# Cross-attention queries as seven half-size block products per head, attention behind all four heads, values by both token tiles per piece

## The chip, the core and the metric

The kernel runs on one core of a Trainium2 chip. Its time is device microseconds. A core has TensorE (matrix products, "PE" in the profile, its weight loads "PEld"), VectorE ("DVE"), ScalarE ("ACT"), GpSimd ("POOL") and SyncE ("SP", which issues most DMAs); the engines run side by side and wait for one another by semaphores. Matrix products go to PSUM, which VectorE and ScalarE read; everything else lies in SBUF.

## The reference

One encoder layer on 512 tokens of width 1024, all in float32, with three parts that each add to x, and a final norm:

```python
x = x + hybrid_mixer(rms_norm(x, norm_mix_g), ...)
x = x + memory_cross_attention(rms_norm(x, norm_xa_g), mem, mem_norm_g, w_q_xa, w_k_xa, w_v_xa, w_o_xa)
x = x + swiglu(rms_norm(x, norm_ffn_g), w_gate_ffn, w_up_ffn, w_down_ffn)
return rms_norm(x, final_g)
```

The change is in the second part. There are 256 memory tokens and 4 heads of 256 columns:

```python
m = rms_norm(mem, mem_g)
q, k, v = h @ wq, m @ wk, m @ wv              # h: 512 x 1024, m: 256 x 1024, weights 1024 x 1024
s = einsum("bqhd,bkhd->bhqk", q, k) * 256 ** -0.5
o = einsum("bhqk,bkhd->bqhd", softmax(s), v)
return o @ wo
```

## The kernel before

**Numbers.** A float32 operand is cut into two parts of a reduced format, a high one (a copy on ACT) and a low one (the rest, a subtraction on DVE); `split` (L101) does it. A product is then three matmul passes, high x high, high x low, low x high (`gemm`, L137). Weights arrive as raw tiles of 1 MB by a DMA on SP's queue into a ring of three (`load_raw`, L111) and are cut into a ring of six pairs (`cut`, L116).

**Order.** Tokens are in four tiles of 128. Instructions are put in order by a planner that works with estimated times; among those ready it goes by the order in which the code writes them. Instructions wrapped in `pin` (L233) keep their written order among themselves on their engine; others may be moved between them.

**Seven products.** The gate projections of the mixer and the gate and up projections of the feed-forward part already use a scheme with seven half-size block products in place of eight (`Seven`, L235, and `seven_run`, L311). An item is 256 weight columns by 512 tokens. Its weights are cut in two along input and output, its activations along input and tokens. The sums of weight blocks are made for each item (two on POOL in `sums`, two on DVE in `sums2`), those of activation blocks once (`r11`, `r21`, `r22` are plain blocks, `t1` to `t4` sums). A product (`mul`, L274) is 12 matmuls of 256 columns. Two accumulators in PSUM take several products one after the other, and copies of states in between (`keep`, L284, on ACT: m1, u2, u3) are added on DVE to give the four blocks of the output: `c11`, `c22`, `c12`, `c21`. `seven_run` is a pipeline over items: in step k it issues five products of item n = k and the last two of item p = k - 1, and prepares the weights of item q = k + 1. All of it is pinned. The accumulators are tiles of a ring of four ("acc"); an item takes two.

**Cross-attention.** After the mixer's output product (`bo`, a `Back`, L853, which leaves normed tokens in `hs`), `norm_turn` (L197) transposes each token tile on PE, multiplies by the gain on DVE and cuts the result into `h2`. Keys go by four loads of 256 columns (L940 to L947), values by two halves of 512 columns through `nat_gemm` (L150), which runs all four pieces of a half for the first token tile and then for the second. Then, head by head, `xa_q` (L958) makes the queries by 48 matmuls of 512 columns and cuts them with the scale, `xa_turn` (L992) transposes the head before, `xa_probs` (L968) makes scores, maximum, exponential and division, `xa_values` (L1001) the weighted values. The output product `bx` starts behind the last head's scores, with that head's transposes and values between its rows.

**Feed-forward.** The tokens are cut into four quarter tiles per part (`h3q`, read through `Quads`, L1037), and the seven-product items of gate and up follow.

Of the kernel before, what the change touches and what calls it, by code (L numbers as in the profile page):

```python
# [8 lines left out]
F32 = mybir.dt.float32  # L9
# [8 lines left out]
def encoder_kernel(  # L18
# [9 lines left out]
    nc = tc.nc  # L28
# [46 lines left out]
    WB = 6  # L75
    chan = cst.tile([P, NC_], F32, name="chan")
    cst.tile([P, 48], F32, name="cpad")
    sm.tile([P, 48], F32, name="spad", bufs=1)
# [155 lines left out]

    class Seven:  # L235


        def __init__(self, src, fp, rights, tile_a):
            self.src, self.fp, self.r, self.tile_a = src, fp, rights, tile_a
# [6 lines left out]
        def sums(self):  # L246

            r = self.raw
            self.s1 = self.fp.tile([P, 4, P], F32, name=nm("s1"), tag="s1", bufs=1)
            pin(nc.gpsimd.tensor_tensor(out=self.s1, in0=r[:, 0:4, P:256], in1=r[:, 4:8, P:256], op=ALU.add))  # L250
            pin(nc.gpsimd.tensor_tensor(out=r[:, 0:4, P:256], in0=r[:, 0:4, 0:P], in1=r[:, 0:4, P:256], op=ALU.subtract))  # L251

        def sums2(self):

# [56 lines left out]
    def seven_run(items, fill=lambda i: None, at=None, then=None):  # L311

        z = len(items)
        for k in range(z + 1):
            n = items[k] if k < z else None
            p = items[k - 1] if k else None
            q = items[k + 1] if k + 1 < z else None
            if k == at:
                got = then()
            if k + 2 < z:  # L320
                items[k + 2].load()
            if n:
# [12 lines left out]
            if p:  # L335
                p.gate22()
                p.mul(p.c, "s4", "r22", False, True)
            if k == z:
                fill(1)
            if q:  # L340
                x = q.hi(("l11", "l12"), q.left)
                q.lo(x)
                c = q.hi(("s1",), q.s1)
            if p:
                p.c12(p.c[:, 0:256], p.u2)
            if n:
# [36 lines left out]
        if z > 1:  # L383
            items[z - 1].extra_out()
        return got if then else None
# [277 lines left out]
    def sgu_v(t, dst):  # L663
        zt = up.tile([P, W], F32, name=nm("zt"), tag="zt", bufs=2)
        nc.scalar.activation(out=zt, in_=dst, func=AF.Gelu)
        st = sm.tile([P, 6], F32, name=nm("st"), tag="st")
        nc.vector.bn_stats(out=st, in_=zt)
        mv = sm.tile([P, 2], F32, name=nm("mv"), tag="mv")
# [184 lines left out]
    class Back:  # L853
# [42 lines left out]
        def half1(self, during=lambda t: None):  # L896
# [3 lines left out]
            for t in range(NT):  # L900
# [3 lines left out]
                    self.step(1, i, t)  # L904
                self.finish(1, t)

    for t in range(NT):
# [42 lines left out]
    close(mp)  # L950
    close(n2)
    close(mtp)


    op_ = pool("op", side="right")
    oT = tuple(op_.tile([P, KD, T], F32R, name=f"oT{s}") for s in "hl")
    qp = pool("qp", side="right")

    def xa_q(h):
        tiles = w_cols(w_q_xa, h * XD)  # L960
        qx = tuple(qp.tile([P, 2, T], F32R, name=nm("qx"), tag=f"qx{s}", bufs=2) for s in "hl")
        for j in range(2):
            dst = bank(nm("pq"))
            col_gemm(dst, tiles[j], h2, ALLT)
            split(dst, qx[0][:, j, :], qx[1][:, j, :], scale=XD ** -0.5)
        return qx

    def xa_probs(h, qx):  # L968
        es = qp.tile([P, NT, NM], F32, name=nm("es"), tag="es", bufs=1)
        for tt in range(2):  # L970
            sc = bank(nm("sc"))
            for u in range(2):
                t = 2 * tt + u
                gemm(sc[:, u * NM:(u + 1) * NM],
                     lambda i: qx[0][:, i, t * P:(t + 1) * P], lambda i: qx[1][:, i, t * P:(t + 1) * P],
                     lambda i: kx[0][:, 2 * h + i, :], lambda i: kx[1][:, 2 * h + i, :], [(0, 0), (1, 1)])
            mx = sm.tile([P, 2], F32, name=nm("mx"), tag="mx")
            nc.vector.tensor_reduce(out=mx, in_=sc.rearrange("p (u m) -> p u m", u=2), axis=AX.X, op=ALU.max)
            nc.vector.tensor_scalar(out=mx, in0=mx, scalar1=-1.0, scalar2=None, op0=ALU.mult)
            su = sm.tile([P, 2], F32, name=nm("su"), tag="su")  # L980
            for u in range(2):
                nc.scalar.activation(out=es[:, 2 * tt + u, :], in_=sc[:, u * NM:(u + 1) * NM], func=AF.Exp,
                                     bias=mx[:, u:u + 1], accum_out=su[:, u:u + 1])
            ri = sm.tile([P, 2], F32, name=nm("ri"), tag="ri")
            nc.vector.reciprocal(out=ri, in_=su)
            for u in range(2):
                t = 2 * tt + u
# [1 line left out]
                                        op0=ALU.mult)  # L989
        return es  # L990

    def xa_turn(es):  # L992
        pT = tuple(qp.tile([P, MT, T], F32R, name=nm("pT"), tag=f"pT{s}", bufs=2) for s in "hl")
        for m in range(MT):
            dst = bank(nm("pT"))
            for t in range(NT):
# [12 lines left out]
    XH = D // XD  # L1009
# [12 lines left out]
    bx.rows(0, 2, 6)  # L1022
    xa_values(XH - 1, pT)
    close(qp)
    close(h2p)
    close(kvp)

    h3p = pool("h3p")
    h3q = [[[None, None] for _ in range(2)] for _ in range(2)]
    for at in ((0, 1, 0), (0, 1, 1), (1, 1, 0), (1, 1, 1), None, (0, 0, 0), (0, 0, 1), (1, 0, 0), (1, 0, 1)):  # L1030
        if at is None:
            h3p.tile([P, 48], F32, name="hpad")
        else:
            u, v, w = at
            h3q[u][v][w] = h3p.tile([P, 4, T // 2], F32R, name=f"h3{'hl'[w]}{u}{v}", tag=f"h3{'hl'[w]}{u}{v}")

    class Quads:  # L1037
        def __init__(self, s):
            self.s = s

        def __getitem__(self, at):
            p, k, c = at
            k, k1 = (k.start, k.stop) if isinstance(k, slice) else (k, None)
            b = c.start // (T // 2)
            c = slice(c.start - b * (T // 2), c.stop - b * (T // 2))
            return h3q[k // 4][b][self.s][p, k % 4 if k1 is None else slice(k % 4, k1 - k + k % 4), c]

    h3 = (Quads(0), Quads(1))
# [425 lines left out]
```

## Time and profile before

| | us |
|---|---|
| median of 3 runs | 961.09 (959.71 to 961.42) |
| the profiled execution, its own time | 961.33 |
| its span, first to last instruction | 959.4 |
| PE busy in the span | 943.3 (98%) |
| DVE busy | 691.9 (72%) |
| ACT busy | 485.4 (51%) |
| POOL busy | 235.2 (25%) |

The span is what the engines' rows cover; the execution's own time holds 1.93 us more around it. A group's row gives line, engine, operation, tiles, shapes and count, then busy time, the mean of one in nanoseconds, and the idle time before. A row of the timeline begins with start and length in microseconds. Matmuls overlap in the pipe, so the time that one costs is read from the distance of starts and not from its length.

### The profile page before, as it was taken

The page shows a single profiled execution, that of the slowest core. Times are in us where ns is not written, and L with a number is a line of the kernel's source. Part 1 is how long each engine was busy: PE and PEld are TensorE (multiplying, and loading weights), DVE is VectorE, ACT ScalarE, POOL GpSimd, SP SyncE. Part 2 cuts the span into 40 slices and gives each one's busy share as a digit, 9 for nine tenths or more (in the row PEclk, how much of TensorE's full clock was granted, in tenths as well). Part 3 has the DMA queues.
Part 4 walks back from the last instruction along what each step waited for, and adds up shares of the span by engine and source line. Part 5 has one row for each costly group of instructions (what it writes and reads, how often), then busy time and mean ns, then how long its engine had stood idle before and what let it go on. Part 6 is the DMA issues. An engine that isn't in the chain of part 4 may idle for free. (4 is left out here: it accounts for less than half of the span.)

```text
span 959.4 us, 14493 instructions
## 1 busy us (share of the span) xinstructions
PE 943.3 (98%) x5894; PEld 849.7 (89%) x5894; DVE 691.9 (72%) x863; ACT 485.4 (51%) x746; POOL 235.2 (25%) x211
## 2 busy tenths in 40 slices
PE   7999999999999999999999999999999999999996
PEld 7988888888999999988988888899999999988885
DVE  6677887658966666566844544598888888777996
ACT  6474665434544344455734433555455545557452
POOL 1221122254411535230000000034544545201001
PEclk8999999999999999999999999999999999999999
DMA  8421212320333323282545121112424242376632
GB/s 289 148 91 44 88 55 78 121 88 22 111 100 120 110 89 110 89 283 67 176 136 172 44 88 44 44 45 89 132 89 133 88 132 89 111 263 138 235 110 87
DMA packets 84275, 109.22 MB, mean 114 GB/s; under 512 B 2177, under 2 KB 63665, under 8 KB 84209
## 3 DMA queue, kind: packets, MB, share of 16 engines
q1 hardware_dynamic: 82384, 101.74, 32.3%
q0 software_dynamic: 1824, 6.55, 2.6%
q8 instruction: 46, 0.75, 0.3%
q14 instruction: 21, 0.16, 0.1%
HBM read 104.10 MB, written 2.10 MB: 111 GB/s over the span
## 5 line engine op out<-in xcount | busy, mean ns | idle before, releaser
L272 DVE TENSOR_TENSOR wl<-wr,wh 128x1024 fp32r<-128x1024 f32 x93 | 135.7, 1470 | 29.4 <-ACT wh L267 29.4
L105 DVE TENSOR_TENSOR wl<-wr,wh 128x1024 fp32r<-128x1024 f32 x80 | 99.7, 1255 | 58.5 <-ACT wh L104 32.7
L104 ACT CAST wh<-wr 128x1024 fp32r<-128x1024 f32 x80 | 82.9, 1050 | 65.8 <-PE pq L142 20.8
L267 ACT CAST wh<-wr 128x1024 fp32r<-128x1024 f32 x93 | 97.8, 1053 | 25.4 <-DVE wr L257 25.4
L174 POOL TENSOR_TENSOR rs<-ve,mhalf 128x1 f32<-128x1 f32 x22 | 14.9, 679 | 304.7 <-DVE ve L172 304.7
L286 ACT COPY u<-pf 128x256 f32<-128x256 f32 x62 | 23.1, 373 | 94.3 <-PE pf L280 31.9
L250 POOL TENSOR_TENSOR s<-wr 128x512 f32<-128x512 f32 x31 | 40.7, 1314 | 115.2 <-DVE w L272 111.1
L251 POOL TENSOR_TENSOR wr<-wr 128x512 f32<-128x512 f32 x31 | 64.6, 2085 | 2.4
L806 POOL TENSOR_TENSOR merged<-merged,sg 128x512 f32<-128x512 f32 x16 | 27.5, 1723 | 79.9 <-DVE sg L805 79.9
L582 POOL TENSOR_SCALAR_AFFINE_SELECT ab<-ab 128x128 f32<-128x128 f32 x32 | 23.8, 777 | 80.1 <-ACT ab L579 80.1
L280 PE MATMUL pf<-h3th,wh 128*128 128x256 f32 x240 | 37.5, 279 | 0.4 <-ACT m L286 0.4
L280 PE MATMUL pf<-h3th,wl 128*128 128x256 f32 x240 | 37.0, 276 | 0.0
L280 PE MATMUL pf<-h3tl,wh 128*128 128x256 f32 x240 | 37.0, 276 | 0.0
L286 ACT COPY m<-pf 128x256 f32<-128x256 f32 x31 | 11.5, 372 | 47.3 <-PE pf L280 45.1
L280 PEld LDWEIGHTS pf<-h3th,wh 128*128 128x128 f32 x240 | 32.2, 189 | 0.7 <-ACT m L286 0.6
L280 PEld LDWEIGHTS pf<-h3tl,wh 128*128 128x128 f32 x240 | 31.7, 188 | 0.0
L280 PEld LDWEIGHTS pf<-h3th,wl 128*128 128x128 f32 x240 | 31.7, 188 | 0.0
L257 DVE TENSOR_TENSOR wr<-wr 128x512 f32<-128x512 f32 x31 | 30.2, 975 | 1.1
L1201 ACT CAST wh<-wr 128x1024 fp32r<-128x1024 f32 x20 | 20.7, 1051 | 18.3 <-PE pc L1170 8.4
L183 ACT ACTIVATE jk<-xr 128x512 f32<-128x512 f32 x24 | 15.2, 631 | 25.6 <-DVE xr L886 13.0
L1127 POOL TENSOR_TENSOR afb<-afb,g 128x256 f32<-128x256 f32 (+1 forms) x16 | 18.4, 1153 | 35.0 <-DVE afb L1100 35.0
L805 DVE TENSOR_TENSOR sg<-pbr,sg 128x512 f32<-128x512 f32 x16 | 11.0, 689 | 20.8 <-PE pbr L798 20.8
(385 smaller groups left out, 2674.8 us busy)
## 6 DMA issues: line engine op xcount, KB each, us to landing
wr<-in_w_in_dram SPq DMA_DIRECT2D x26, 1024.0 KB, 5.1
wr<-in_w_down_ffn_dram SPq DMA_DIRECT2D x13, 1024.0 KB, 5.5
wr<-in_w_gate_ffn_dram SPq DMA_DIRECT2D x11, 1024.0 KB, 5.4
wr<-in_w_up_ffn_dram SPq DMA_DIRECT2D x11, 1024.0 KB, 5.4
wb<-in_w_branch_dram SPq DMA_DIRECT2D x12, 512.0 KB, 3.4
wr<-in_w_out_dram SPq DMA_DIRECT2D x4, 1024.0 KB, 8.2
wr<-in_w_k_xa_dram SPq DMA_DIRECT2D x4, 1024.0 KB, 8.0
wr<-in_w_v_xa_dram SPq DMA_DIRECT2D x4, 1024.0 KB, 5.1
```

The costliest lines, as they stand in the source:

```text
L104: nc.scalar.copy(out=hi, in_=src)
L105: nc.vector.tensor_tensor(out=lo, in0=src, in1=hi, op=ALU.subtract)
L250: pin(nc.gpsimd.tensor_tensor(out=self.s1, in0=r[:, 0:4, P:256], in1=r[:, 4:8, P:256], op=ALU.add))
L251: pin(nc.gpsimd.tensor_tensor(out=r[:, 0:4, P:256], in0=r[:, 0:4, 0:P], in1=r[:, 0:4, P:256], op=ALU.subtract))
L257: pin(nc.vector.tensor_tensor(out=r[:, 4:8, 0:P], in0=r[:, 4:8, 0:P], in1=r[:, 0:4, 0:P], op=ALU.subtract))
L267: pin(nc.scalar.copy(out=t[0], in_=src))
L272: pin(nc.vector.tensor_tensor(out=l, in0=src, in1=h, op=ALU.subtract))
L280: pin(nc.tensor.matmul(dst[:, 0:256], w[:, k, :], v[:, k, :], start=first and n == 0, stop=last and n == 11, skip_group_check=True))
L286: pin(nc.scalar.copy(out=m, in_=self.a[:, 0:256]))
L582: nc.gpsimd.affine_select(out=dg, in_=dg, compare_op=ALU.is_gt, fill=0.0, base=0, channel_multiplier=1, pattern=[[-1, P]])
L806: pin(nc.gpsimd.tensor_tensor(out=merged[:, d, :], in0=merged[:, d, :], in1=sg, op=ALU.add))
L1201: pin(nc.scalar.copy(out=hi, in_=src))
```

## The change

Queries become four items of the seven-product scheme (`Query`, one per head), run by `seven_run`. For that the normed tokens are kept in quarter tiles `h2q` (a function `quads`, which now also makes `h3q`); the plain block r12 isn't needed in cut form, and its tiles hold the raw block first and then the items' weight sums. `query_turn` takes the place of `norm_turn`, and `query_forms`, called for token tiles 2 and 3, makes the sums t1 to t4 into `h2t`. The outputs of an item are copied (`put`) and later cut (`rest`) into `qx`, one pair of tiles per head; the scale 256 ** -0.5 moves into the exponential. In `seven_run`, the copy u2 is written behind `sums2`, and a new step `out12` (empty for the other classes) follows it. The run's two fill places, ahead of the last two products, hold the scores of heads 0 and 1; heads 2 and 3, all transposes and all values follow the run, and rows of the output product stand between the last two heads' parts. The value projection runs both token tiles for each piece of weights, and the first two heads' loads and head 0's preparation are written behind the second half's matmuls. Probabilities and their transposes lie in tiles of `h2p` that are free by then. A pad and some small buffers become smaller.

```diff
@@ class Seven, seven_run
+        eng = nc.gpsimd
...
-        extra_cut = extra_mul = extra_out = extra_load
+        extra_cut = extra_mul = extra_out = out12 = extra_load
...
             if n:
                 n.mul(n.a, "s2", "t2", False, False)
-                n.u2 = n.keep("u2")
             if q:
                 q.sums2()
+            if n:
+                n.u2 = n.keep("u2")
+            if p:
+                p.out12()
+            if q:
                 q.lo(c)
@@ tokens
-    h2 = tuple(h2p.tile([P, KD, T], F32R, name=f"h2{s}") for s in "hl")
+    h2q = quads(h2p, "h2", F32)
...
-    bo.half1(lambda t: t > 0 and norm_turn(n2, hs[t - 1], G_XA, h2, t - 1))
+    def query_turn(t):
+        i, ts = t // 2, slice(t % 2 * P, (t % 2 + 1) * P)
+        for g in range(2):
...
+            hf = n2.tile([P, 4, P], F32, name=nm("hf"), tag="hf", bufs=2) if i else h2q[0][1][g][:, :, ts]
...
+            nc.vector.tensor_tensor(out=hf, in0=pt.rearrange("p (j c) -> p j c", j=4), in1=gv, op=ALU.mult)
+            if g or not i:
+                split(hf, *(v[:, :, ts] for v in h2q[g][i]))
+
+    def query_forms(t):
+        f = n2.tile([P, 2, 4, P], F32, name=nm("h"), tag="h", bufs=2)
...
+        for n, (p, q, o) in enumerate(((r12, r11, r22), (r22, r12, r21))):
+            if n:
+                nc.vector.tensor_tensor(out=f[:, 1], in0=o, in1=f[:, 1], op=ALU.subtract)
+            nc.vector.tensor_tensor(out=f[:, 0], in0=p, in1=q, op=ALU.subtract)
+            if not n:
+                nc.vector.tensor_tensor(out=f[:, 1], in0=o, in1=f[:, 0], op=ALU.subtract)
...
+            split(f, h2t[0][sl], h2t[1][sl])
+
+    bo.half1(lambda t: t > 0 and query_turn(t - 1))
...
+    query_forms(NT - 2)
@@ keys
         if c == 1:
-            norm_turn(n2, hs[NT - 1], G_XA, h2, NT - 1)
+            query_turn(NT - 1)
+            query_forms(NT - 1)
@@ queries
+    acc = lambda: psm.tile([P, 512], F32, name=nm("pf"), tag="acc", bufs=4)
...
+    class Query(Seven):
...
+        def put(self, j, i, src):
+            hi, lo = (v[:, j, HT[i]] for v in qx[self.h])
+            pin(nc.scalar.copy(out=hi, in_=src))
+            self.due[j, i] = (lo, src, hi)
+        def rest(self, j, i):
+            lo, src, hi = self.due.pop((j, i))
+            pin(nc.vector.tensor_tensor(out=lo, in0=src, in1=hi, op=ALU.subtract))
+        def c11(self, p, m):
+            self.add(p, m)
+            self.put(0, 0, m)
+        def c22(self, p, m):
+            self.add(p, m)
+            self.rest(0, 0)
+            self.put(1, 1, m)
+        def gate22(self):
+            self.rest(1, 1)
+        def c12(self, p, m):
+            self.add(p, m)
+            self.m12 = m
+        def out12(self):
+            self.put(0, 1, self.m12)
+        def done0(self):
+            self.rest(0, 1)
+        def c21(self, p):
+            self.put(1, 0, p)
+        def extra_mul(self):
+            self.rest(1, 0)
@@ values and the order behind them
-    for cs in HALVES:
-        nat_gemm(w_v_xa, cs.start, mT, MT, lambda t, dst: split(dst, vx[0][:, t, cs], vx[1][:, t, cs]))
+    for n, cs in enumerate(HALVES):
+        dsts = [bank(nm("pn")) for t in range(MT)]
+        for c in range(2):
+            for i, pc in enumerate(w_rows(w_v_xa, 4 * c, 4, cs.start)):
+                k = 4 * c + 2 * i
+                for t in range(MT):
+                    gemm(dsts[t],
...
+                         [(k, 0), (k + 1, 1)], first=k == 0, last=k == KD - 2)
+        if n:
+            seven_open(qs)
...
-    es = xa_probs(0, xa_q(0))
-    for h in range(1, XH):
-        qx = xa_q(h)
-        nT = xa_turn(es)
-        es = xa_probs(h, qx)
-        xa_values(h - 1, nT)
+    seven_run(qs, probs)
...
+    turn(0)
+    probs(2)
+    xa_values(0, pT[0])
+    turn(1)
+    probs(3)
+    xa_values(1, pT[1])
     bx.start()
     bx.rows(0, 0, 2)
-    pT = xa_turn(es)
-    bx.rows(0, 2, 6)
-    xa_values(XH - 1, pT)
+    turn(2)
+    bx.rows(0, 2, 4)
+    xa_values(2, pT[2])
+    turn(3)
+    bx.rows(0, 4, 6)
+    xa_values(3, pT[3])
```

More of the change, by code (lines that the diff above doesn't have):

```diff
@@ L249, in sums @@
             self.s1 = self.fp.tile([P, 4, P], F32, name=nm("s1"), tag="s1", bufs=1)
-            pin(nc.gpsimd.tensor_tensor(out=self.s1, in0=r[:, 0:4, P:256], in1=r[:, 4:8, P:256], op=ALU.add))
-            pin(nc.gpsimd.tensor_tensor(out=r[:, 0:4, P:256], in0=r[:, 0:4, 0:P], in1=r[:, 0:4, P:256], op=ALU.subtract))
+            pin(self.eng.tensor_tensor(out=self.s1, in0=r[:, 0:4, P:256], in1=r[:, 4:8, P:256], op=ALU.add))
+            pin(self.eng.tensor_tensor(out=r[:, 0:4, P:256], in0=r[:, 0:4, 0:P], in1=r[:, 0:4, P:256], op=ALU.subtract))
         def sums2(self):
@@ L905, in half1, with quads, __init__, __getitem__ @@
                 self.finish(1, t)
+    def quads(p, name, first=F32R):
+        q = [[[None, None] for _ in range(2)] for _ in range(2)]
+        for at in ((0, 1, 0), (0, 1, 1), (1, 1, 0), (1, 1, 1), None, (0, 0, 0), (0, 0, 1), (1, 0, 0), (1, 0, 1)):
+            if at is None:
+                p.tile([P, 48], F32, name=f"{name}pad")
+            else:
+                u, v, w = at
+                n = f"{name}{'hl'[w]}{u}{v}"
+                q[u][v][w] = p.tile([P, 4, T // 2], first if v > u else F32R, name=n, tag=n)
+        return q
+    class Quads:
+        def __init__(self, q, s):
+            self.q, self.s = q, s
+        def __getitem__(self, at):
+            p, k, c = at
+            k, k1 = (k.start, k.stop) if isinstance(k, slice) else (k, None)
+            b = c.start // (T // 2)
+            c = slice(c.start - b * (T // 2), c.stop - b * (T // 2))
+            return self.q[k // 4][b][self.s][p, k % 4 if k1 is None else slice(k % 4, k1 - k + k % 4), c]
     for t in range(NT):
@@ L946, in encoder_kernel @@
         if c == 1:
-            norm_turn(n2, hs[NT - 1], G_XA, h2, NT - 1)
-    for cs in HALVES:
-        nat_gemm(w_v_xa, cs.start, mT, MT, lambda t, dst: split(dst, vx[0][:, t, cs], vx[1][:, t, cs]))
[L950 to L966, printed above, removed]
@@ L968, in xa_probs, with tile @@
-    def xa_probs(h, qx):
-        es = qp.tile([P, NT, NM], F32, name=nm("es"), tag="es", bufs=1)
+            query_turn(NT - 1)
+            query_forms(NT - 1)
+    XH = D // XD
+    class Room:
+        def tile(self, shape, dtype, name, tag, bufs):
+            if tag == "s1":
+                return h2p.tile(shape, dtype, name=name, tag="h2h01")
+            if tag == "w2h":
+                self.both = h2p.tile([shape[0], 2] + shape[1:], dtype, name=name, tag="h2l01")
+                return self.both[:, 0]
+            if tag == "w2l":
+                return self.both[:, 1]
+            return fq.tile(shape, dtype, name=name, tag=tag, bufs=2)
@@ new lines, in encoder_kernel, with __init__, add @@
+    acc = lambda: psm.tile([P, 512], F32, name=nm("pf"), tag="acc", bufs=4)
+    qrights = dict(r11=h2q[0][0], r21=h2q[1][0], r22=h2q[1][1])
+    for i, n in enumerate((1, 2, 3, 4)):
+        qrights[f"t{n}"] = tuple(v[:, i] for v in h2t)
+    class Query(Seven):
+        def __init__(self, h):
+            super().__init__(w_q_xa[:, h * XD:(h + 1) * XD], room, qrights, acc)
+            self.h, self.due = h, {}
+        def put(self, j, i, src):
[5 more added lines that the diff above has]
+            pin(nc.vector.tensor_tensor(out=lo, in0=src, in1=hi, op=ALU.subtract))
+        def add(self, p, m):
+            pin(nc.vector.tensor_tensor(out=m, in0=p, in1=m, op=ALU.add))
+        def c11(self, p, m):
[18 more added lines that the diff above has]
+            self.rest(1, 0)
@@ L970, in xa_probs @@
+    room = Room()
+    qs = [Query(h) for h in range(XH)]
+    SC = XD ** -0.5
+    def xa_probs(h):
+        es = h2p.tile([P, NT, NM], F32, name=nm("es"), tag=f"h2{'hl'[h % 2]}00")
         for tt in range(2):
@@ L974, in xa_probs @@
                 gemm(sc[:, u * NM:(u + 1) * NM],
[L975 removed]
+                     lambda i: qx[h][0][:, i, t * P:(t + 1) * P], lambda i: qx[h][1][:, i, t * P:(t + 1) * P],
                      lambda i: kx[0][:, 2 * h + i, :], lambda i: kx[1][:, 2 * h + i, :], [(0, 0), (1, 1)])
[L977 removed]
+            mx = sm.tile([P, 2], F32, name=nm("mx"), tag="mx", bufs=3)
             nc.vector.tensor_reduce(out=mx, in_=sc.rearrange("p (u m) -> p u m", u=2), axis=AX.X, op=ALU.max)
[L979 to L980 removed]
+            nc.vector.tensor_scalar(out=mx, in0=mx, scalar1=-SC, scalar2=None, op0=ALU.mult)
+            su = sm.tile([P, 2], F32, name=nm("su"), tag="su", bufs=3)
             for u in range(2):
                 nc.scalar.activation(out=es[:, 2 * tt + u, :], in_=sc[:, u * NM:(u + 1) * NM], func=AF.Exp,
[L983 to L984 removed]
+                                     bias=mx[:, u:u + 1], scale=SC, accum_out=su[:, u:u + 1])
+            ri = sm.tile([P, 2], F32, name=nm("ri"), tag="ri", bufs=3)
             nc.vector.reciprocal(out=ri, in_=su)
@@ L990, in xa_probs, with xa_turn @@
         return es
-    def xa_turn(es):
-        pT = tuple(qp.tile([P, MT, T], F32R, name=nm("pT"), tag=f"pT{s}", bufs=2) for s in "hl")
+    def xa_turn(h, es):
+        pT = tuple(h2p.tile([P, MT, T], F32R, name=nm("pT"), tag=f"h2{s}{1 if h % 2 else 0}1") for s in "hl")
         for m in range(MT):
@@ L1007, in xa_values, with probs, turn @@
             split(dst, oT[0][:, dt_, :], oT[1][:, dt_, :])
-    XH = D // XD
-    es = xa_probs(0, xa_q(0))
-    for h in range(1, XH):
-        qx = xa_q(h)
-        nT = xa_turn(es)
-        es = xa_probs(h, qx)
-        xa_values(h - 1, nT)
+    ess = {}
+    def probs(h):
+        ess[h] = xa_probs(h)
+    for n, cs in enumerate(HALVES):
[5 more added lines that the diff above has]
+                    gemm(dsts[t],
+                         lambda a: mT[0][:, a, t * P:(t + 1) * P], lambda a: mT[1][:, a, t * P:(t + 1) * P],
+                         lambda a: pc[0][:, a, :], lambda a: pc[1][:, a, :],
+                         [(k, 0), (k + 1, 1)], first=k == 0, last=k == KD - 2)
+        if n:
+            seven_open(qs)
+        for t in range(MT):
+            split(dsts[t], vx[0][:, t, cs], vx[1][:, t, cs])
+    close(mp)
+    close(n2)
+    qxp = pool("qxp")
+    qx = [tuple(qxp.tile([P, 2, T], F32R, name=f"qx{s}{h}") for s in "hl") for h in range(XH)]
+    fq = pool("fq")
+    seven_run(qs, probs)
+    close(fq)
+    close(h2tp)
+    op_ = pool("op", side="right")
+    oT = tuple(op_.tile([P, KD, T], F32R, name=f"oT{s}") for s in "hl")
+    pT = {}
+    def turn(h):
+        pT[h] = xa_turn(h, ess[h])
     h3p_done = {}
     bx = Back(w_o_xa, oT, KD, KD, lambda t, half: h3p_done["f"](t, half))
+    turn(0)
[4 more added lines that the diff above has]
+    xa_values(1, pT[1])
     bx.start()
     bx.rows(0, 0, 2)
-    pT = xa_turn(es)
-    bx.rows(0, 2, 6)
-    xa_values(XH - 1, pT)
-    close(qp)
+    turn(2)
[4 more added lines that the diff above has]
+    xa_values(3, pT[3])
+    close(qxp)
     close(h2p)
@@ L1028, in encoder_kernel @@
     h3p = pool("h3p")
[L1029 to L1048, printed above, removed]
+    h3q = quads(h3p, "h3")
+    h3 = tuple(Quads(h3q, i) for i in range(2))
     h3t = tuple(h3p.tile([P, 4, 4, T // 2], F32R, name=f"h3t{s}") for s in "hl")
```

20 lines of the change are left out of this document (17 added, 3 removed).

## The prediction

> **What bounds the kernel now.** I read the page's busy line first, then the busy time of each engine in the stretches that the change touches (columns: stretch, length, then busy time and instructions of PE, PEld, DVE, ACT, POOL, the granted clock, the DMA share, GB/s), then PE's waits there.
>
> ```profile
> span 959.4 us, 14493 instructions
> PE 943.3 (98%) x5894; PEld 849.7 (89%) x5894; DVE 691.9 (72%) x863; ACT 485.4 (51%) x746; POOL 235.2 (25%) x211
> ...
> 461.00:485.75 24.75, 24.75 (x209) 24.75 (x208) 19.68 (x28) 15.77 (x25) 1.40 (x1) 1.00 0.58 190
> 485.75:507.50 21.75, 21.75 (x98) 18.03 (x97) 8.18 (x9) 6.84 (x10) 0.00 (x0) 1.00 0.52 171
> 507.50:594.40 86.90, 86.38 (x441) 73.24 (x440) 44.33 (x78) 37.15 (x72) 0.00 (x0) 1.00 0.26 85
> ...
> PE sc L142 <- DVE qx L108: 0.5, 1, 0.5
> ```
>
> TensorE is busy through keys (461 to 485.75), values (to 507.5) and attention (to 594.4), at full clock; its only wait there is 0.5 us before one score. VectorE (DVE) is half idle in the last stretch. So time is won here only by fewer matmul columns, and lost by any new TensorE wait. The profiled execution took 961.33 us, 1.93 more than its span and 0.24 above the median of 961.09; the sum is made against 961.33 and 0.24 is taken off at the end.
>
> **The products.** Today four heads of queries take 192 matmuls of 512 columns. Their price is the spacing of their starts, since durations overlap. First the queries, then the feed-forward stage, which already runs seven half-size products per item, then the keys, the slowest 256-column product near by:
>
> ```profile
> L142 PE MATMUL pq<-h2h,wl 128*128 128x512 f32 x64 | 16.0, 390 | 0.0
> ...
> 541.32 1.98 PE L142 MATMUL pq<-h2l,wh 128*128 128x512 f32 x8
> 543.13 1.98 PE L142 MATMUL pq<-h2h,wl 128*128 128x512 f32 x8
> ```
> ```profile
> 685.48 0.62 PE L280 MATMUL pf<-h3th,wl 128*128 128x256 f32 x4
> 685.93 0.62 PE L280 MATMUL pf<-h3h,wh 128*128 128x256 f32 x4
> ...
> 695.53 0.62 PE L280 MATMUL pf<-h3h,wh 128*128 128x256 f32 x4
> ```
> ```profile
> 475.19 1.12 PE L142 MATMUL pk<-mTl,wh 128*128 128x256 f32 x8
> 476.15 1.12 PE L142 MATMUL pk<-mTh,wl 128*128 128x256 f32 x8
> ```
>
> Eight 512-column matmuls take 543.13 - 541.32 = 1.81 us, so a head takes 6 x 1.81 = 10.88 us and four take 43.5. An item of seven products (84 matmuls) takes 695.53 - 685.93 = 9.60 us; four take 38.4. **Saved: 5.1 us.** At the keys' pace (0.96 us for eight, 0.12 each) an item would take 10.08 and the saving be 3.2; that is the lower bound. I take 9.60, because the new query tiles are cut into the same quarters as that stage's. Scores, transposes, values and the output product keep their matmuls. The old 0.5 us wait goes too, since its query is long ready when the scores come: **0.5 saved**.
>
> **Work that moves and is hidden.** Each of the two calls of query_forms adds four 128x512 subtractions and two 128x1024 cuts on DVE. Their prices, and when the keys' weights are cut and needed:
>
> ```profile
> 627.99 0.68 DVE L223 TENSOR_TENSOR tf<-hf,hf 128x512 f32<-128x512 f32 x1
> ...
> L105 DVE TENSOR_TENSOR wl<-wr,wh 128x1024 fp32r<-128x1024 f32 x16 | 19.4, 1222 | 9.3 <-ACT wh L104 9.3
> L105 DVE TENSOR_TENSOR h2l<-hf,h2h 128x512 fp32r<-128x512 f32 x6 | 4.1, 687 | 0.1
> ...
> 473.74 1.23 DVE L105 TENSOR_TENSOR wl<-wr,wh 128x1024 fp32r<-128x1024 f32 x1 [0.97 <-ACT wh L104]
> ```
> ```profile
> 482.87 1.12 PE L142 MATMUL pk<-mTh,wh 128*128 128x256 f32 x8
> ```
>
> 4 x 0.68 + 2 x 1.22 = 5.2 us a call, 10.3 in all; two 0.7 us cuts of the block that is no longer needed go. Head 0's preparation adds two subtractions, one half-size cut and one full cut, 3.3 us. DVE has 46.5 - 19.68 - 8.18 = 18.6 us free from 461 to 507.5 and is asked for 12.2 more. The last key weights are cut at 473.74 and first read at 482.87, nine microseconds ahead, so the delay shows nowhere. Taking both token tiles per piece of the value weights gives each piece 12 matmuls, 2.7 us, instead of 1.36 us, so late cuts are excused there too. I price all this at nothing; without the cover it is at most the 3.8 us by which 19.68 + 10.3 - 1.4 overruns the keys' 24.75. The loads on SP's queue are the same four of 1 MB, asked for earlier. The two extra sums a head on GpSimd (POOL) meet an idle engine.
>
> **The new wait.** Each step of the pinned run ends on DVE with: add for c11 (head n), add for c22 (head n), cut of block 00 (head n), and only then, in extra_mul, the cut of block 10 of head n-1, which reads that head's first accumulator in PSUM. There are four such buffers and each head takes two, so the first product of head n+1 reuses exactly that buffer and waits for that last cut. TensorE's pinned order has nothing after product s3t3 to do meanwhile. In the feed-forward stage the accumulator is read earlier. Its rows around the same place (the step begins at 685.93), with the busy times of that step first:
>
> ```profile
> 685.93:695.53 9.60, 9.60 (x86) 9.60 (x85) 8.34 (x11) 4.49 (x7) 5.49 (x4) 1.00 0.36 109
> ...
> 684.77 1.93 DVE L272 TENSOR_TENSOR wl<-wr,wh 128x1024 fp32r<-128x1024 f32 x1 [0.52 <-ACT wh L267]
> 686.63 0.41 DVE L1100 TENSOR_TENSOR af<-pfb,m 128x256 f32<-128x256 f32 x1
> 687.56 0.42 DVE L1100 TENSOR_TENSOR af<-pf,u 128x256 f32<-128x256 f32 x1 [0.52 <-ACT u L286]
> ```
> ```profile
> 687.15 0.37 ACT L286 COPY u<-pf 128x256 f32<-128x256 f32 x1 [2.13 <-DVE af L1100]
> 687.42 1.06 ACT L267 CAST wh<-wr 128x1024 fp32r<-128x1024 f32 x1
> ```
>
> The shortest chain, DVE being on time: s3t3's last matmul ends at 685.48 + 0.62 = 686.10, 0.17 after the point where the next product could start; ACT copies u3 (0.37), then DVE adds c22, cuts 00, cuts 10 (0.34, 0.34, 0.42 with starts overlapping by 0.08), and three hops of about 0.05 to 0.1 (0.04 from ACT's end at 687.52 to DVE at 687.56): 1.8 us. But DVE is late here already: the c11 add begins 0.70 behind the step. Then the copy for block 00 (ACT, 0.37) comes ahead of u3's copy on ACT, and the chain runs 0.70 + 0.41 + 0.3 + 0.4 + 0.34 + 0.34 + 0.42 + hops = 3.0 us. Step 0 holds only five products, 5/7 x 9.60 = 6.9 us, while DVE has nearly the 8.34 us of a whole step to do; I put 0.8 for the part of that lag that is still there at head 2. So head 2 waits 1.8 to **3.8 us**; I take 3.8, as the queue runs late in the nearest rows. At head 3 DVE has had that pause to catch up: **1.8**. Head 1 takes unused buffers, and after head 3 the scores come. Together 5.6.
>
> Can anything fill it? The score matmuls of head 0 aren't pinned, and unpinned work does pass work written earlier in this kernel: scores start between two query products, and the first up-product's multiplication (L1156) stands ahead of a pinned cut that the code writes before it:
>
> ```profile
> 518.42 0.40 PE L142 MATMUL sc<-kxh,qx 128*128 128x256 f32 x2
> 518.65 2.00 PE L142 MATMUL pq<-h2h,wh 128*128 128x512 f32 x8
> ...
> 647.02 0.69 DVE L1156 TENSOR_TENSOR af<-pf,g 128x512 f32<-128x512 f32 x1 [0.39 <-PE pf L142]
> 647.63 1.46 DVE L272 TENSOR_TENSOR wl<-wr,wh 128x1024 fp32r<-128x1024 f32 x1
> ```
>
> At head 2's wait, the scores of head 0's last two token tiles are ready: 12 x 0.12 = 1.4 us, brought forward at no cost. At head 3's, the rest of head 0's are, which covers 1.8. So 3.8 - 1.4 = **2.4 us** of waiting stays, between 0 (if DVE is on time) and 5.6 (if nothing is brought forward).
>
> **Attention behind the queries.** A block of scores goes through a maximum, two exponentials and two scalings before its transposes:
>
> ```profile
> L978 DVE TENSOR_REDUCE mx<-sc 128x2 f32<-128x512 f32 x8 | 5.5, 692 | 13.6 <-PE sc L142 13.6
> L988 DVE TENSOR_SCALAR es<-es,ri 128x256 f32<-128x256 f32 x16 | 4.9, 351 | 0.1
> ```
> ```profile
> L982 ACT ACTIVATE es<-sc,mx 128x256 f32<-128x256 f32 x16 | 7.4, 471 | 15.5 <-DVE mx L979 15.5
> ```
>
> That is 0.69 + 2 x 0.47 + 2 x 0.35 = 2.3 us and some small steps. Score work of two heads (24 x 0.12 = 2.9 us each) and two products of 1.36 lie between head 0's first score and its transposes, 8.5 us; behind them each head's transposes are followed by another head's scores before its values. Nothing waits, as now: 0, with the old 0.5 as upper bound.
>
> **Sum:** -5.1 - 0.5 + 2.4 = -3.2, so 961.33 - 3.2 = 958.1, and 957.9 as a median.
>
> **The rivals.** (1) *Nothing fills the waits*: -5.1 - 0.5 + 5.6 = 0, 961.1. For it: the queue is pinned by hand; against it: the overtaking above. (2) *The unfilled wait slows the clock*, slower than before. The start of this kernel shows what a pause does: PE waited 3.8 us, and the clock (third figure from the right) fell.
>
> ```profile
> 8.00:12.00 4.00, 0.16 (x2) 0.12 (x1) 3.37 (x4) 3.56 (x8) 0.00 (x0) 0.79 1.08 362
> 12.00:16.00 4.00, 4.00 (x19) 4.00 (x20) 4.00 (x9) 2.97 (x5) 0.93 (x1) 0.50 0.77 262
> 16.00:20.00 4.00, 4.00 (x32) 4.00 (x32) 2.50 (x7) 2.65 (x9) 0.09 (x1) 0.86 1.02 327
> ...
> PE pv L142 <- ACT hTh L104: 3.8, 1, 3.8
> ```
>
> Lost: 4 x 0.50 + 4 x 0.14 = 2.6 us. Head 2's wait of 3.8 is as long; with this behind it, rival (1) becomes 963.7. It decides from a wait somewhere between 0.5 us (the one before the scores, at a clock of 1.00) and 3.8; against it: the fill shortens the wait to 2.4. [...] (3) *Everything is covered*: DVE on time, waits of 1.8 wholly filled: -5.6, 955.5. Against it: DVE's rows stand late. (4) *Slow columns*: the keys' 0.12 for the new products; -3.2 - 0.5 + 2.4 = -1.3, 959.8. For it: the same shape does run at two paces.
>
> **How the numbers follow.** Forecast 0.45 (own range 956.4 to 959.2), (1) 0.20, (2) 0.14, (3) 0.12, (4) 0.09. A measurement of this kernel can tell about 0.2%, 1.9 us, from no change; so 959.2 divides faster from same and 963.0 same from slower. Faster: forecast and (3), 0.56; same: (1), (4) and the forecast's edge, 0.28; slower: 0.16. The range runs from 955.3, just below (3), to 963.2, which leaves out most of (2).
>
> **What would show it.** Four items of about 9.6 us, 84 matmuls each, under the queries' line; PE idle before the first product of heads 2 and 3, released by DVE's block-10 cut; scores of head 0 inside the query run; no PE idle from 461 to 507. Wrong if PE doesn't wait there, if the products run near 0.12, if the clock dips behind the wait, or if keys or values wait on their cuts.

## The result and the profile after

The changed kernel takes 953.93 us (median of six runs, 953.23 to 954.58). The kernel before took 960.17 in six runs, of which the three shown ahead of the prediction were 961.09 in the median. The ratio is 0.9933, 95% interval 0.992 to 0.9945: faster by 6.2 us, and the slowest of the new runs (954.58) is below the fastest of the old (959.71). The forecast was 957.9 with a range down to 955.3, so the time lies 4.0 below the forecast and 1.4 below the range. The profiled execution of the changed kernel took 953.87 us.

The busy line of the changed kernel, and then all of PE's waits from 455 to 618 us in it:

```profile
span 952.2 us, 14860 instructions
PE 935.4 (98%) x6038; PEld 849.3 (89%) x6038; DVE 720.6 (76%) x909; ACT 498.5 (52%) x776; POOL 248.6 (26%) x219
```
```profile
PE pf L282 <- DVE qxl L1043: 0.2, 1, 0.2
```

TensorE is still the engine that sets the time, and the forecast's 2.4 us of waiting are 0.2. The same three stretches as before, by engine (columns as in the prediction), show that DVE did take up the work that moved (16.96 us busy in the second stretch, 8.18 before) and that PE has no idle time in the first two:

```profile
461.00:485.75 24.75, 24.75 (x200) 23.96 (x199) 22.79 (x33) 15.78 (x24) 1.39 (x1) 1.00 0.67 210
485.75:507.50 21.75, 21.75 (x115) 18.55 (x114) 16.96 (x19) 9.97 (x15) 6.38 (x4) 1.00 0.31 100
507.50:594.40 86.90, 86.64 (x600) 79.61 (x600) 63.33 (x116) 47.59 (x100) 7.01 (x4) 1.00 0.30 98
```

To compare the two, I measure one stretch in each: from the first key product to the feed-forward part's first product. PE's timeline, before:

```profile
460.99 0.88 PE L142 MATMUL pk<-mTh,wh 128*128 128x256 f32 x6
624.38 1.07 PE L142 MATMUL pf<-h3h,wh 128*128 128x256 f32 x7
```

and after, with three more places that are used below:

```profile
459.85 0.88 PE L142 MATMUL pk<-mTh,wh 128*128 128x256 f32 x6
...
478.20 0.63 PE L142 MATMUL pn<-wh,mTh 128*128 128x512 f32 x2
...
482.40 1.09 PE L142 MATMUL pk<-mTh,wh 128*128 128x256 f32 x8
...
522.14 0.62 PE L282 MATMUL pf<-h2h,wh 128*128 128x256 f32 x4
...
523.50 0.39 PE L142 MATMUL sc<-kxh,qxh 128*128 128x256 f32 x2
...
526.02 0.72 PE L282 MATMUL pf<-h2th,w 128*128 128x256 f32 x4 [0.15 <-DVE qxl L1043]
...
617.18 1.07 PE L142 MATMUL pf<-h3h,wh 128*128 128x256 f32 x7
```

The stretch took 624.38 - 460.99 = 163.39 us and takes 617.18 - 459.85 = 157.33: **6.06 less**, nearly all of the 6.24 between the medians. Summing the distances from each PE row's start to the next, by what the row makes, accounts for all of it:

| PE work in the stretch | before, us | after, us | difference | forecast |
|---|---|---|---|---|
| keys | 23.26 | 22.32 | -0.94 | 0 |
| values | 21.80 | 22.05 | +0.25 | 0 |
| query products | 43.58 | 39.03 | -4.55 | -5.1 |
| scores, and the waits filled by them | 12.46 | 11.94 | -0.52 | -0.5 + 2.4 |
| transposes, weighted values, output product | 62.29 | 61.99 | -0.30 | 0 |

Outside the stretch the two profiled executions differ by 1.4 us more, most of it ahead of the part that changed: the first query product of the mixer starts at 40.27 before and at 39.11 after. In the other runs below, each a single one, that mark lies between 38.1 and 40.1 in kernels whose code up to there is the same, save for one padding in the last of them. So I take this for the spread of the program's start (the changed kernel itself gave 39.11 and 39.53), and compare the kernels below by the stretch, not by their whole time. The kernel before and the changed one, run again as experiments, gave 163.09 (with one padding) and 157.23.

### The profile page after: what moved, and what is told of

It is laid out like the page before. It is cut to its first block, busy times and chain, and to the rows that moved or that the text cites. A ratio compares the mean times of both kernels' runs of the same rounds, so it can differ in the third digit from the quotient of the medians.

```text
span 952.2 us, 14860 instructions
## 1 busy us (share of the span) xinstructions
PE 935.4 (98%) x6038; PEld 849.3 (89%) x6038; DVE 720.6 (76%) x909; ACT 498.5 (52%) x776; POOL 248.6 (26%) x219
## 5 line engine op out<-in xcount | busy, mean ns | idle before, releaser
L274 DVE TENSOR_TENSOR wl<-wr,wh 128x1024 fp32r<-128x1024 f32 x105 | 152.6, 1463 | 32.2 <-ACT wh L269 32.2
L269 ACT CAST wh<-wr 128x1024 fp32r<-128x1024 f32 x105 | 110.4, 1053 | 30.3 <-DVE wr L259 30.3
L105 DVE TENSOR_TENSOR wl<-wr,wh 128x1024 fp32r<-128x1024 f32 x72 | 89.9, 1257 | 33.9 <-ACT wh L104 24.0
L104 ACT CAST wh<-wr 128x1024 fp32r<-128x1024 f32 x72 | 74.7, 1050 | 48.2 <-PE pb L142 18.2
L252 POOL TENSOR_TENSOR s<-wr 128x512 f32<-128x512 f32 x35 | 46.0, 1315 | 157.5 <-DVE w L274 135.4
L288 ACT COPY u<-pf 128x256 f32<-128x256 f32 x70 | 26.1, 373 | 98.3 <-PE pf L282 35.0
L253 POOL TENSOR_TENSOR wr<-wr 128x512 f32<-128x512 f32 x35 | 72.7, 2077 | 2.7
L259 DVE TENSOR_TENSOR wr<-wr 128x512 f32<-128x512 f32 x35 | 33.0, 942 | 1.2
L1330 ACT CAST wh<-wr 128x1024 fp32r<-128x1024 f32 x20 | 20.7, 1052 | 18.4 <-PE pc L1299 9.2
L258 DVE TENSOR_TENSOR wr<-s,wr 128x512 f32<-128x512 f32 x35 | 23.9, 683 | 4.7 <-POOL wr L253 4.3
```

Source lines behind the costliest of these rows:

```text
L104: nc.scalar.copy(out=hi, in_=src)
L105: nc.vector.tensor_tensor(out=lo, in0=src, in1=hi, op=ALU.subtract)
L252: pin(self.eng.tensor_tensor(out=self.s1, in0=r[:, 0:4, P:256], in1=r[:, 4:8, P:256], op=ALU.add))
L253: pin(self.eng.tensor_tensor(out=r[:, 0:4, P:256], in0=r[:, 0:4, 0:P], in1=r[:, 0:4, P:256], op=ALU.subtract))
L258: pin(nc.vector.tensor_tensor(out=r[:, 0:4, 0:P], in0=self.s1, in1=r[:, 0:4, 0:P], op=ALU.subtract))
L259: pin(nc.vector.tensor_tensor(out=r[:, 4:8, 0:P], in0=r[:, 4:8, 0:P], in1=r[:, 0:4, 0:P], op=ALU.subtract))
```

## The experiments

Theory, after the result: the late cut exists as forecast, but the wait moved by one product and was filled. The forecast had assumed that accumulators go round in a fixed turn. Rivals: DVE was simply on time; or filling has no part in it. Separately: why the keys became faster, and whether the moved work is hidden wherever it stands.

**Accumulators in a fixed turn.** The four accumulators of the query items are handed out in a fixed order:

```diff
+    def turns():
+        if len(ring) < 4:
+            ring.append(acc())
+        else:
+            ring.append(ring[-4])
+        return ring[-1]
-            super().__init__(w_q_xa[:, h * XD:(h + 1) * XD], room, qrights, acc)
+            super().__init__(w_q_xa[:, h * XD:(h + 1) * XD], room, qrights, turns)
```

> The changed kernel, with the four accumulator buffers of the query products handed out in fixed turn, so that the first product of head n+1 gets the buffer that is freed last. Stage = start of the first key product to start of the first feed-forward product; 157.3 us in the changed kernel, 163.4 before. Theory (the planner gives a head's first accumulator the buffer that comes free first, which moved the wait one product later, and scores filled the rest): TensorE now finds nothing of its own order at the first product of head 2, 3 to 4 us of waiting of which about 17 scores (2 us) are filled, and 1 to 2 us at head 3; stage 1.5 to 2.5 us longer. Rival (VectorE is on time, there is no wait to speak of): no change, stage within 0.3 us.

Measured: 956.15 us, the stretch 160.14, which is 2.81 more than the changed kernel. PE's timeline of this run:

```profile
523.59 0.51 PE L142 MATMUL sc<-kxh,qxh 128*128 128x256 f32 x2 [1.31 <-DVE m L1055]
...
525.42 0.73 PE L282 MATMUL pf<-h2h,wh 128*128 128x256 f32 x4 [0.15 <-DVE qxl L1052]
...
536.95 0.74 PE L282 MATMUL pf<-h2h,wh 128*128 128x256 f32 x4 [0.85 <-DVE qxl L1052]
```

Head 2's first product (525.42) and head 3's (536.95) now wait for the late cut, partly filled by scores, and 1.31 + 0.15 + 0.85 = 2.31 us of idle time remain. The sum is the forecast's 2.4, under the condition that the forecast had taken for granted, but that it fits so well is partly luck: 1.46 us of it stand at head 2, where the forecast had 2.4, and 0.85 at head 3, which it had as covered. A further 0.4 us is idle behind the query items, ahead of a weighted-values product.

**Scores pinned.** The matmuls of heads 0 and 1's scores keep their written place, so that they can't be brought forward:

```diff
-                nc.tensor.matmul(dst, a(i), b(j), start=first and n == 0, stop=last and n == tot - 1)
+                keep(nc.tensor.matmul(dst, a(i), b(j), start=first and n == 0, stop=last and n == tot - 1))
...
-                     lambda i: kx[0][:, 2 * h + i, :], lambda i: kx[1][:, 2 * h + i, :], [(0, 0), (1, 1)])
+                     lambda i: kx[0][:, 2 * h + i, :], lambda i: kx[1][:, 2 * h + i, :], [(0, 0), (1, 1)],
+                     keep=pin if h < 2 else lambda i: None)
```

> The changed kernel, with the score matmuls of heads 0 and 1 kept in written order behind the third step, so that nothing can fill a wait in the query run. Theory: the wait of 2.5 us ahead of head 2's second product and one of about 0.5 us at head 3 now stand open: PE idle 2.5 to 3 us there, stage 2 to 3 us longer than 157.3. Rival (no wait): no change, since scores then only move back to where they are written.

Measured: 958.16 us, the stretch 160.75 (+3.42). PE's timeline and then a stretch behind the first wait by engine:

```profile
526.84 0.72 PE L282 MATMUL pf<-h2th,w 128*128 128x256 f32 x4 [2.36 <-DVE qxl L1043]
...
536.99 0.74 PE L282 MATMUL pf<-h2th,w 128*128 128x256 f32 x4 [0.28 <-DVE qxl L1043]
```
```profile
527.00:531.00 4.00, 4.00 (x36) 4.00 (x37) 3.46 (x5) 2.25 (x4) 0.00 (x0) 1.00 0.23 43
```

So DVE isn't on time: without the fill PE idles 2.36 us, at the head's *second* accumulator (its product streams h2t, as in the changed kernel). The clock stays at 1.00.

**Both together.**

> Both together: buffers in fixed turn and scores kept in written order. This is the case that the forecast's first rival described. By the forecast's chain: waits of 3.8 us at head 2 and 1.8 at head 3, stage 5 to 6 us longer than 157.3, and, if a pause of this length slows the clock, a granted clock below 1.00 behind it and up to 2.6 us more. Rival (no wait): no change.

Measured: 961.92 us, the stretch 164.99 (+7.66). PE's timeline, then three stretches by engine:

```profile
526.33 0.74 PE L282 MATMUL pf<-h2h,wh 128*128 128x256 f32 x4 [3.69 <-DVE qxl L1052]
...
539.45 0.72 PE L282 MATMUL pf<-h2h,wh 128*128 128x256 f32 x4 [1.64 <-DVE qxl L1052]
```
```profile
523.00:527.00 4.00, 0.68 (x5) 0.68 (x6) 2.53 (x5) 2.03 (x4) 2.15 (x2) 1.00 0.00 0
527.00:531.00 4.00, 4.00 (x24) 4.00 (x23) 2.79 (x3) 1.59 (x3) 0.00 (x0) 0.59 0.34 101
531.00:535.00 4.00, 4.00 (x36) 4.00 (x35) 2.58 (x5) 1.58 (x4) 0.00 (x0) 0.98 0.43 165
```

This is the forecast's bare chain: 3.69 and 1.64 us against 3.8 and 1.8. Behind the long wait the clock fell to 0.59 for 4 us, which costs, by an estimate from these clocks, 4 x 0.41 + 4 x 0.02 = 1.7 us: rival (2)'s slowed clock does occur, behind a wait of 3.69 us and not behind one of 2.36 (the run before).

**The late cut taken away.** The cut of block 10 moves from the last step of the pipeline to `c21`, right behind its high part:

```diff
         def c21(self, p):
             self.put(1, 0, p)
-
-        def extra_mul(self):
             self.rest(1, 0)
```

> The changed kernel with the cut of head n-1's block 10 done in order, right behind its product, so that no head's accumulators wait for one that is freed late. Theory A (as the planner hands out the accumulators, only some 0.2 us of waiting is left, and the filling scores were needed work in any case): within 0.4 us of the changed kernel, 953.5 to 954.3, with no wait of a product for an accumulator. Theory B (the late cut still costs what its fill displaces): 1 to 2 us faster, near 952.5.

Measured: 955.51 us, the stretch 159.03, 1.70 **more**. Neither theory foresaw that. ACT's timeline of this run, then the PE row that waits:

```profile
535.85 1.28 ACT L1092 ACT_TABLE_LOAD   x1
...
539.25 1.06 ACT L269 CAST wh<-wr 128x1024 fp32r<-128x1024 f32 x1
540.20 1.06 ACT L104 CAST wh<-wr 128x1024 fp32r<-128x1024 f32 x1
541.14 0.39 ACT L288 COPY m<-pf 128x256 f32<-128x256 f32 x1
```
```profile
538.97 1.45 PE L1107 MATMUL pT<-ident,es 128*128 128x128 f32 x8 [0.42 <-DVE es L1098]
541.58 0.74 PE L282 MATMUL pf<-h2th,wh 128*128 128x256 f32 x4 [1.17 <-ACT m L288]
```

No product waits for an accumulator any more, but head 0's scores are now done by 527.36, and its softmax, with its table load, starts on ACT at 535.85, ahead of head 3's copy m1. In the changed kernel that load stands at 540.45, behind the same copy (538.23). The copy comes late, and 1.17 us are idle at a product, and 0.42 at the transposes that the planner also brought forward. The cut's lateness was cheap because scores filled it; what came in its place was dearer.

**The keys.** In the compiled programs, which give each tile its address, mT (the memory's transpose) lies elsewhere in the changed kernel than in the one before, because of the new tiles. Either that place made the keys faster or the other work around them did. First the kernel before with 192 bytes of padding ahead of mT:

```diff
     h2 = tuple(h2p.tile([P, KD, T], F32R, name=f"h2{s}") for s in "hl")
+    h2p.tile([P, 48], F32, name="h2pad")
```

> [...] Rival (keys are faster in the changed kernel because other work around them moved): still 0.120.

Measured: 960.91 us; the keys took 22.50 us instead of 23.26, but the values 22.32 instead of 21.80; the stretch 163.09 (-0.30). Then the opposite, the changed kernel with 64 bytes of padding ahead of mT (`mp.tile([P, 16], F32, name="mpad")`) and nothing else, to bring the old pace back:

> [...] Theory A (the 0.9 us that the key stage gained come from where mT lies against the weights): the key products go back from 0.113 to about 0.120 us each, 22.3 us to about 23.2, and the kernel from 953.9 to about 954.6. Theory B (they come from the changed order, in which value products stand between the key products): the keys stay at 22.3 us, and the time at 953.9.

Measured: 955.33 us; the keys 23.27 us, the values 21.82, the stretch 158.04 (+0.71). The keys' rows of the changed kernel, then of this run:

```profile
464.41 1.07 PE L142 MATMUL pk<-mTl,wh 128*128 128x256 f32 x8
465.32 1.07 PE L142 MATMUL pk<-mTh,wl 128*128 128x256 f32 x8
```
```profile
464.32 1.12 PE L142 MATMUL pk<-mTh,wh 128*128 128x256 f32 x8
465.28 1.12 PE L142 MATMUL pk<-mTl,wh 128*128 128x256 f32 x8
```

Eight take 0.91 us or 0.96, by where the streamed tile lies (the six groups of eight from 472.46 to 478.20 of the changed kernel are slower than its others, 0.94 to 1.03). With mT 64 bytes further on the keys take what they took before the change (23.27, 23.26), so nothing of their 0.94 us needs the new order.

**The order of the values, and the place of the preparation.** The values as before the change, one token tile after the other, with the query items opened (`seven_open`: two loads, the first head's sums and cuts) behind them:

```diff
-    for n, cs in enumerate(HALVES):
-        dsts = [bank(nm("pn")) for t in range(MT)]
...
+    for cs in HALVES:
+        nat_gemm(w_v_xa, cs.start, mT, MT, lambda t, dst: split(dst, vx[0][:, t, cs], vx[1][:, t, cs]))
+    seven_open(qs)
```

> The changed kernel with the values as before (one token tile after the other in each half of the columns, each with its own pass over the pieces), and the quads of the queries opened behind them. Theory A (the order of the values is cover alone): within 0.5 us of the changed kernel, 953.9. Theory B (the value products that both tiles share per piece are what filled the time in which the last key cuts were late): PE is idle for 1 us or more between the key products, and the time is about 955 to 956.

Measured: 961.20 us, the stretch 163.91 (+6.58): the whole gain gone, but with no idle time between key products. The edit had changed two things, so they were tried one by one. The old value order with the opening ahead of the last half's splits, where the changed kernel has it:

```diff
+    def evac(t, dst, n, cs):
+        if n and t == 0:
+            seven_open(qs)
+        split(dst, vx[0][:, t, cs], vx[1][:, t, cs])
...
+        nat_gemm(w_v_xa, cs.start, mT, MT, lambda t, dst: evac(t, dst, n, cs))
```

> The changed kernel with the values as before the change, one token tile after the other in each half of the columns, but with the quads of the first two heads loaded and prepared ahead of the last half's splits, as the changed kernel does. Theory A (what the run with the old value order lost, 6.6 us between the first key product and the feed-forward block, is the late preparation of the first head's weights, not the order of the value products): within 1 us of the changed kernel in that stretch, 157 to 158.5 us, about 954.5 in all. Theory B (the order of the value products itself is what let the weights be cut in time): 160 us or more in that stretch, 957 or more in all.

Measured: 954.00 us, the stretch 157.26 (-0.07). And the new value order with the opening behind the last splits:

```diff
-        if n:
-            seven_open(qs)
         for t in range(MT):
             split(dsts[t], vx[0][:, t, cs], vx[1][:, t, cs])
+    seven_open(qs)
```

> The changed kernel with its own order of the value products, but with the quads of the first two heads loaded and prepared only behind the last half's splits. Theory A (the place of the preparation decides): the first products of head 0 wait for their cut weights, 4 us or more are lost, 959 or more in all. Theory B (the value order decides): within 1 us of the changed kernel, about 954.5.

Measured: 960.00 us, the stretch 163.99 (+6.66). The order of the values is worth nothing here; two lines' place in the program is worth as much as the change. ACT's timeline of this run, then of the changed kernel:

```profile
505.33 0.59 ACT L104 CAST vxh<-pn 128x512 fp32r<-128x512 f32 x1 [0.79 <-PE pn L142]
505.81 1.05 ACT L269 CAST wh<-wr 128x1024 fp32r<-128x1024 f32 x1
```
```profile
493.16 1.04 ACT L269 CAST wh<-wr 128x1024 fp32r<-128x1024 f32 x1
```

Written behind the last splits, head 0's weight cut waits for the last value product; written ahead of them it comes 13 us earlier. PE's waits in the run with the opening behind show the price:

```profile
PE pf L282 <- DVE u L1046: 1.9, 1, 1.9
PE pf L282 <- ACT wh L269: 1.6, 1, 1.6
PE pf L282 <- ACT m L288: 1.0, 1, 1.0
PE pf L282 <- DVE w L274: 0.4, 1, 0.4
PE pf L282 <- DVE qxl L1043: 0.2, 1, 0.2
```

Head 0's products wait for its weights and the first state copy (1.6, 0.4, 1.0), and at 521.02 head 0's block 22 product waits 1.9 us for an addition on DVE, which is behind: 4.9 of the 6.7 us. The other 1.8 lie in shorter gaps at the same products, by the distances of starts.

**The products' pace.** The twelve matmuls per item that stream block 22 ran at 0.118 us in the changed kernel. To see whether the place of those tiles sets that pace, the 192 bytes of padding among the quads were moved ahead of them, so that they lie 192 bytes further on:

```diff
-        for at in ((0, 1, 0), (0, 1, 1), (1, 1, 0), (1, 1, 1), None, (0, 0, 0), (0, 0, 1), (1, 0, 0), (1, 0, 1)):
+        for at in ((0, 1, 0), (0, 1, 1), None, (1, 1, 0), (1, 1, 1), (0, 0, 0), (0, 0, 1), (1, 0, 0), (1, 0, 1)):
```

> [...]

Measured: 956.85 us. The block 22 products of heads 0 and 1 did become fast with their tiles moved (eight in 0.91 us, from 514.33). But the four query items gained nothing by it (39.00 us, 39.03 in the changed kernel), because a slow stretch of 17 us came among other products (from 528.27), and 3.75 us were lost in the feed-forward part (330.32 us from the start of its first product to the start of PE's last row, 326.57 in the changed kernel). PE's timeline of this run there:

```profile
688.86 0.62 PE L282 MATMUL pf<-h3tl,w 128*128 128x256 f32 x4
689.31 0.62 PE L282 MATMUL pf<-h3th,w 128*128 128x256 f32 x4
689.87 0.74 PE L282 MATMUL pf<-h3h,wh 128*128 128x256 f32 x4
690.44 0.63 PE L282 MATMUL pf<-h3l,wh 128*128 128x256 f32 x4
690.91 0.64 PE L282 MATMUL pf<-h3h,wl 128*128 128x256 f32 x4
691.39 0.63 PE L282 MATMUL pf<-h3th,wh 128*128 128x256 f32 x4
```

At 689.87 there is a gap of 0.1 us (0.56 instead of 0.45 between starts), and behind it four matmuls take 0.47 us instead of 0.45, whichever tiles they stream, up to 835 us, with the granted clock at 1.00. So the place of the tiles isn't the only cause of the slow pace. There is a second one, which here began behind a small gap and lasted; that the gap started it isn't shown. The changed kernel, run again, was to show whether it comes by chance:

> The changed kernel once more, on this chip. From the first key product to the feed-forward block's first product 157.3 us as before, to 0.3. Theory A (the runs of query products at 0.118 us instead of 0.113 are set by where the tiles lie): the same products are slow again. Theory B (the pace is a state that TensorE falls into behind a short gap and keeps for a while): the slow stretches begin and end elsewhere, and the time moves by up to 1 us with them.

Measured: 954.31 us, the stretch 157.23. In the query stage a slow stretch (0.117 to 0.120 us a matmul) begins at the same product in both runs, head 1's block 22 product in head 2's step (at 527.49 and 527.98), and ends in head 3's item some 10 us later, one product earlier in the second run; so its start doesn't come by chance. In the feed-forward part single slow products differ between the two, at no difference in time (326.61 and 326.57 us). And with hT moved as well, by 192 bytes of padding ahead of it in place of those behind it, to see whether the places alone set the pace:

> [...] Theory A (the pace of 0.118 us comes only from where the tiles lie): about 4 us less than the changed kernel, near 950. [...]

Measured: 957.46 us. The feed-forward part has no long slow stretch here (326.19 us, 0.4 less than the changed kernel), with its tiles placed as in the run that had one; but 4.5 us were lost between the first mixer product and the keys (425.24 us instead of 420.74), where hT and what is allocated behind it are streamed. So the expectation didn't hold (957.46 us, not near 950): what starts the lasting slow pace stays open, and no placing of these tiles that beats the changed kernel was found.

## Why the prediction was wrong

**The products: right, the size off.** "Saved: 5.1 us" measured 4.55: an item takes 39.03 / 4 = 9.76 us and not 9.60, because block 22's matmuls and a stretch of some 10 us behind one of them run at 0.118 us. What causes that pace here stays open: with block 22's tiles moved, the four items took the same 39.00. The value lies between the two bounds given (3.2 and 5.1). Rival (4), the keys' 0.12 throughout, is not what happens.

**The old score wait: right.** It is gone.

**The new wait: the step that failed.** The sentence was "the first product of head n+1 reuses exactly that buffer and waits for that last cut". The late chain itself was right. DVE's rows of the changed kernel:

```profile
523.72 0.41 DVE L1046 TENSOR_TENSOR m<-pfb,m 128x256 f32<-128x256 f32 x1
524.87 0.42 DVE L1046 TENSOR_TENSOR u<-pf,u 128x256 f32<-128x256 f32 x1 [0.74 <-ACT u L288]
525.21 0.42 DVE L1043 TENSOR_TENSOR qxl<-m,qxh 128x256 fp32r<-128x256 f32 x1
525.54 0.42 DVE L1043 TENSOR_TENSOR qxl<-pf,qxh 128x256 fp32r<-128x256 f32 x1
```

From head 2's start at 522.14 to the end of the last cut at 525.96 are 3.8 us, the forecast's figure, in the forecast's order; the first addition begins 1.58 us behind that start, where the forecast had 0.70 + 0.8. But the accumulators don't go round in a fixed turn. In the compiled program head 2's first one takes the PSUM bank that head 0's second one left, which is free early, and its second one takes the bank of the late cut. So the first product runs at once (522.14 to 523.50), and only the second one waits: 526.02 - 523.50 = 2.5 us, in which 17 scores of head 0 are done that were due anyway, about 2.0 us of work. Some 0.5 us is lost where the forecast had 2.4, and at head 3 nothing. The forecast's fill of 12 scores was too small, and its start 1.4 us too early. The two runs that restore one condition each (a fixed turn, pinned scores) give back 2.8 and 3.4 of the stretch's 6.06 us, and both together 7.7 (1.7 of it by the clock), so the gain rests on the turn and on the fill. The range reached down to "Everything is covered" at 955.3, but only with DVE on time as its reason.

**The hidden work: nothing lost, as forecast, but with a row misread.** The cut at 473.74 is not the last one of the key weights. In the compiled program, whose DVE instructions match the trace's rows one by one, it belongs to the second piece of the value weights. The low part of the last key weights is cut at 468.84 before the change and at 467.09 after it:

```profile
468.84 1.22 DVE L105 TENSOR_TENSOR wl<-wr,wh 128x1024 fp32r<-128x1024 f32 x1
```
```profile
467.09 1.22 DVE L105 TENSOR_TENSOR wl<-wr,wh 128x1024 fp32r<-128x1024 f32 x1
```

It is first read at 484.79 before and at 486.95 after, 16 and 20 us later, so the cover was larger than "nine microseconds". The planner did put 18 value products ahead of the last two groups of keys (478.20 to 482.40); the cuts were no reason for that, and why it did stays open. The bound "at most the 3.8 us" was too narrow: it counted the sums of query_forms alone, and with the preparation of head 0 written behind the splits 6.7 us are lost. The forecast had priced the amount of DVE work, not its place in the queues.

**The keys and the values: not seen.** The new tiles shifted mT, and with it the keys' pace: -0.94 and +0.25. The forecast had the keys' pace as a row (0.96 for eight) and used it only as a bound for the new products.

**Attention: right.** -0.30 instead of 0, with no wait.

Of the 2.9 us by which the stretch beat the forecast, the accumulators and their fill are 1.9, keys and values 0.7, the rest of the scores' row about 0.5 (they run at 0.116 us each instead of 0.119, which makes some 0.3; the remainder lies in short gaps), attention 0.3, less the 0.55 that the products fell short. Another 0.9 of the 4.0 is that the median of before moved from 961.09 to 960.17 with three more runs.

**The rivals.** (1) and (2) didn't occur, since they need the fixed turn and no fill; the run with both shows them, at 961.92, between their 961.1 and 963.7. (3) is nearest, 955.5, but by the wrong mechanism: DVE was as late as forecast. The granted clock was 1.00 behind the wait of 2.36 us (scores pinned, 527 to 531 us) and 0.59 behind that of 3.69 us (both together, the same 4 us).

## What to carry to other kernels

Before pricing a wait for a buffer, find out which buffer the product really gets: with a pool that hands out what is free first, as this one did, a late reader delays the second taker and not the first, and the time of a whole product, with any unpinned work behind it, stands ahead of the wait. Price the preparation of a new stage by where it stands in its engines' queues and not by the engine's spare time; here two lines' place was worth 6.7 us, more than the columns saved. A change that adds or removes tiles also moves all that is allocated behind them, and can shift the pace of matmuls that it doesn't touch; here the keys took 0.94 us less and the values 0.25 more.

## What the runs showed of the hardware

A 256-column matmul has two paces here, 0.113 and 0.118 to 0.120 us, at a granted clock of 1.00. One cause is where the operands lie: moving the streamed tile mT by 192 bytes, with no other edit, took eight key products from 0.96 to 0.91 us in the kernel before, and moving it by 64 bytes from 0.91 back to 0.96 in the changed one. In the mixer of the changed kernel the pace differs with the loaded operand, the weight sums `w` or the weights `wh` and `wl`, at the same streamed tiles:

```profile
360.55 0.64 PE L282 MATMUL pf<-hTtl,w 128*128 128x256 f32 x4
361.02 0.64 PE L282 MATMUL pf<-hTth,w 128*128 128x256 f32 x4
...
363.40 0.62 PE L282 MATMUL pf<-hTtl,wh 128*128 128x256 f32 x4
363.85 0.62 PE L282 MATMUL pf<-hTth,wl 128*128 128x256 f32 x4
```

Four take 0.47 us with `w` and 0.45 with `wh`. What makes one place slow and another fast isn't shown, and none of these places of mT was the best for both of its uses: 512 columns wide, with mT as the loaded operand, the values take 21.80 us in the kernel before and 22.32 with the 192 bytes, 22.05 in the changed kernel and 21.82 with the 64.

A second cause of the slow pace wasn't found out. In one run it began behind a gap of 0.1 us and lasted for 145 us at a granted clock of 1.00; in the run with the opening behind, a wait of 1.01 us (at 512.04) was followed by four matmuls in 0.45.
